# Lo parts of the attention keys or queries kept on both partition halves, in a two-block transformer kernel on one Trainium2 core

## The chip, the core and the metric

The kernel runs on one core of a Trainium2 chip. Its time is the device time of one execution in microseconds (us), taken as the median of several runs; lower is better.

## The reference, cut to what matters

Batch 1, 512 tokens, model width 1024, all in float32. A first block mixes a linear recurrence with a dilated attention of 8 heads; a second block of two layers follows, each with an attention mixer and a mixture of 16 experts. The even layer's mixer has 4 differential heads (two score sets each) and 8 grouped-query heads over 512 tokens plus 256 context tokens; the odd layer's has 16 heads whose score is a sum of a 64-wide and a 32-wide product. All scores are products over a head dimension of 64:

```python
def diff_attend(q, k, v, lam, scale):
    s = jnp.einsum('bqhcd,bkhcd->bhcqk', q, k).astype(jnp.float32) * scale
...
def gqa_attend(q, k, v, scale):
    s = jnp.einsum('bqhgd,bkhd->bhgqk', q, k).astype(jnp.float32) * scale
...
def mla_attend(qn, qr, kn, kr, v, scale):
    s = jnp.einsum('bqhd,bkhd->bhqk', qn, kn) + jnp.einsum('bqhr,bkr->bhqk', qr, kr)
```

## The kernel before

**Split products.** Large products are made of parts: a value w becomes hi, its copy in the type fp32r, and lo = w - hi, also fp32r. A dense product is three matmuls, hi by hi, hi by lo and lo by hi (`mm3`, L318 to L320). In the attention, with a head dimension of 64, the two parts of a vector lie one above the other on the 128 partitions that a matmul contracts over.

**Stacks.** `stack_pair` (L456) puts, for two heads, hi on one partition half and lo on the other. `stack_keys` (L484) takes the other operand of two heads: `kh[j]` holds the hi part of head j twice, on both halves (two ScalarE copies, L493 and L494), while `kl` holds the lo parts of both heads in one tile, head 0 on the lower half and head 1 on the upper (one VectorE subtraction each, L495). `dup_head` (L468) does the same for one key head that several query heads share, but writes its lo part on both halves (L475, L476); the grouped-query heads use it.

**Scores.** A unit is one head (or one of the two score sets of a differential head) of one tile of 128 queries. Its scores are sums of passes in PSUM (`scores`, L497 to L504, keys in chunks of 512 and 256): the full stack against the doubled hi part (128 rows: hi times hi and lo times hi), then only the half of the stack that holds hi against the lo part (64 rows). The odd layer has a third pass, the 32-wide product, also 128 rows (`qp`, `krs`), and there queries and keys have changed roles: the stack is `ks`, the lo tile is `ql`. The first block writes the two passes out by itself (L817, L818).

```python
passes.append(((qh[b], ks[b]), (ql[sl], ks[b][sl]), (qp[b], krs)))
```

**What follows the scores.** VectorE takes the maximum (L511), ScalarE the exponential (L514), TensorE transposes the result (L525, copied out at L252 or L254), and TensorE multiplies by the values (L533 or L1146). `Pipe` emits the later steps of a unit two units behind its scores. At the same time `weave` spreads the next heads' projections (L318 to L320, evacuated by ScalarE), their norms and stacks, and matmuls for the modulation vectors (L359, weights streamed by DMA) between the attention steps. The engines' final orders come from a scheduler at build time.

**Between the stages.** The end of each attention loads the out-projection's weights (`resident_`, L305): eight rows `wo_raw` [128, 1024] through two buffers, each split by ScalarE (L267) and GpSimd (L268). Behind them on the same SP queue are the first loads of the experts' weights (`we`, L1418, 1 MB each). Then come the out-projection with the router, and the experts. The order of the program is: first block (0 to 415 us of the profile), even mixer (415 to 873), its out-projection (to about 1000), experts (to 1600), odd mixer (1600 to 1985, attention from 1670), its out-projection, experts (2080 to the end).

Of the kernel before, what the change touches and what calls it, by code (L numbers as in the profile page):

```python
# [19 lines left out]
D = 1024  # L20
# [82 lines left out]
class Pipe:  # L103
    """Units of work in three stages, the later stages emitted `lag` units after the first."""
# [20 lines left out]
def weave(*streams):  # L125
    """Steps of several (generator, its number of steps), spread evenly."""
    live = [[0.5 / max(n, 1), 1.0 / max(n, 1), g] for g, n in streams]
    while live:
        x = min(live, key=lambda z: z[0])
        if next(x[2], True) is None:  # L130
            x[0] += x[1]
            yield
        else:
            live.remove(x)
# [7 lines left out]
def drain(gen):  # L142
    """Runs gen; returns what it returns."""
# [14 lines left out]
class Kernel:  # L158
# [20 lines left out]
    def pbank(self):  # L179
        """A bank that may be held between steps."""  # L180
# [46 lines left out]
    def rsqrt(self, ssq, n, scale, eps=EPS, engine=None, tag="rs"):  # L227
        """1 / sqrt(ssq * scale + eps) [128, n] by Newton's iteration, on VectorE or mostly on another engine."""
# [19 lines left out]
    def evac(self, out, ps, act=4, of=6):  # L248
        """PSUM to SBUF, on ScalarE in `act` of `of` cases."""
# [20 lines left out]
    def group_(self, src):  # L270
        """The parts of a group of weights, in steps of one piece; each is split two steps after its load."""
# [25 lines left out]
    def transposed_(self, ps, hT, w, c0):  # L297
        """transposed() into ps, in two steps"""
# [6 lines left out]
    def resident_(self, src, pool, js, out, mod=8, raw=None):  # L305
        """The rows js (tiles of 128) of src [128, 8, 1024], split, to out[j], in steps."""
        for j in js:
            i = j % mod
            w = (raw or pool).tile([128, D], F32, name="wo_raw", tag="xr", bufs=2)
            self.nc.sync.dma_start(out=w, in_=src[:, j, :])  # L310
            hi, lo = (pool.tile([128, D], F32R, name=f"wo_{nm}{i}", bufs=1) for nm in ("hi", "lo"))
            self.split(hi, lo, w)
# [9 lines left out]
    def natural_(self, ps, h, w, c0, n):  # L322
        """ps [128 tokens, n] = h @ w[:, c0:c0+n], in two steps; h: the two parts [128, k, 128 tokens]."""
# [7 lines left out]
    def ada(self, w, b, stat, nmod, nvec, pool, ring, banks, done, bank=None, bufs=None):  # L331
        """Steps; done(mods, rows) is called with every two modulations' rows: rows holds at partition
        32 t + m the columns (4 bank + t) * 512 of vector m."""
# [34 lines left out]
    def ada_cols(self, rows, n, dst, mods, nvec):  # L368
        """dst[:, m, j, :] = the 8 columns of modulation mods[j] of vector m."""
# [23 lines left out]
    def ada2(self, i):  # L393
        """Modulation of layer i: columns of the mixer's scale and shift, the rows in DRAM, and the
        steps of some banks of it."""
# [20 lines left out]
    def tile_rstd(self, x, junk):  # L416
        """1 / rms of the rows of x [128, 1024]; junk: a tile to write over."""
# [4 lines left out]
    def normalise(self, xs, xn, junk):  # L422
        """Two token tiles [128, 1024] to xn; junk: a tile to write over."""
# [8 lines left out]
    def build_hT(self, xn, A, B, hi, lo, pool):  # L432
        """Two normalised token tiles, modulated, transposed and split, to hi and lo [128, 8, 256]."""
# [22 lines left out]
    def stack_pair(self, S0, S1, nat, ntt, bank=None):  # L456
        """nat(t) [128 tokens, 2 heads x 64]: S0 = hi | lo of the first head, S1 = lo | hi of the second."""
# [10 lines left out]
    def dup_head(self, H, L, ps, r, s):  # L468
        """H, L [128, .]: twice the hi and twice the lo parts of ps, on partitions r.."""
# [14 lines left out]
    def stack_keys(self, kh, kl, nat, ntt, bank=None):  # L484
        """nat(t) [128 tokens, 2 heads x 64]: kh[j] = twice the hi part of head j, kl = the lo parts of both."""
        a_, v = self.nc.scalar, self.nc.vector
        for t0 in range(0, ntt, 4)[::-1]:
# [3 lines left out]
            for j in range(2):  # L491
                q, o = slice(64 * j, 64 * j + 64), slice(64 - 64 * j, 128 - 64 * j)
                a_.activation(kh[j][q, s], ps[q], AF.Copy)  # L493
                a_.activation(kh[j][o, s], ps[q], AF.Copy)  # L494
                v.tensor_sub(kl[q, s], ps[q], kh[j][q, s])  # L495

    def scores(self, passes, q0, k0, k1):  # L497
        """PSUM [128 queries from q0, keys k0..k1] summed over pairs (query stack, key stack)."""
# [1326 lines left out]
```

## Time and profile before

| | |
|---|---|
| median of 3 runs | 2590.11 us (2589.2 to 2593.87) |
| profiled execution | span 2592.4 us |
| TensorE (PE) busy | 2247.1 us, 87% |
| VectorE (DVE) busy | 1052.2 us, 41% |
| ScalarE (ACT) busy | 710.7 us, 27% |
| GpSimd (POOL) busy | 580.7 us, 22% |
| mean granted TensorE clock | 0.928 of full speed |

The span runs from the first to the last instruction of the profiled execution; no time of its own beyond the span is given for it, and it lies within the three runs. PE is the matmul, PEld the load of its stationary operand, which may run beside another matmul. A matmul's recorded duration contains its latency, so consecutive rows overlap; the pace of TensorE is read from the distance between starts.

### The profile page before, as it was taken

The numbers are of one execution on the slowest core, as the hardware profiler recorded it, in microseconds if no ns is written. First come the engines' busy times: TensorE is split into PE (matmuls) and PEld (weight loads), VectorE is DVE, ScalarE is ACT, GpSimd is POOL, SyncE is SP. The second block draws the span as 40 slices with busy tenths as digits, with TensorE's granted clock in tenths as the row PEclk, the third lists the DMA queues.
The fourth block names the chain that finished last, engine by engine and source line by source line (L and its number), as shares of the span: only waits on it lengthen the run. The fifth ranks groups of instructions, "written<-read, shape, count | busy, mean of one in ns | idle before, by whom it ended". The sixth has DMA issues, their size and how long they took to land.

```text
span 2592.4 us, 32517 instructions
## 1 busy us (share of the span) xinstructions
PE 2247.1 (87%) x12298; PEld 1226.4 (47%) x12298; DVE 1052.2 (41%) x2745; ACT 710.7 (27%) x1626; POOL 580.7 (22%) x788
## 2 busy tenths in 40 slices
PE   5999878999999986999999996699999688776777
PEld 1767667676777771222222224466666532222222
DVE  5365677544767653111111116777673610000000
ACT  3355543334544320000000004345555100000000
POOL 3343231331333321011111003333233110000000
PEclk7999888998998897999999998699999889998889
DMA  7531231322332458999999953032214699999997
GB/s 276 163 115 41 78 122 42 122 71 69 113 94 75 162 206 292 383 382 377 377 377 383 388 189 94 21 98 83 70 42 141 253 348 389 397 396 397 389 402 283
DMA packets 158456, 563.85 MB, mean 217 GB/s; under 512 B 16198, under 2 KB 16454, under 8 KB 158172
## 3 DMA queue, kind: packets, MB, share of 16 engines
q1 hardware_dynamic: 143868, 522.90, 54.2%
q0 software_dynamic: 14432, 38.88, 5.5%
q8 instruction: 97, 1.59, 0.2%
q14 instruction: 59, 0.48, 0.1%
HBM read 538.59 MB, written 23.14 MB: 217 GB/s over the span
## 4 chain that ended last, share of the span: by engine, by line
PE 39%; DMA 14%; DVE 5%; ACT 3%; issue 3%; POOL 0%; SPq 0%; POOLq 0%; ACTq 0%; DVEq 0%
PE bank L1470 12%; DMA we<-in_w_exp_gate_dram 9%; PE pbank L1505 5%; PE bank L503 5%; PE bank L1461 5%; DMA we<-in_w_exp_up_dram 4%; PE pbank L1520 2%; PE bank L533 2%; PE bank L525 1%; PE pbank L318 1%; PE pbank L320 1%; PE pbank L359 1%; PE pbank L319 1%; PE pbank L1316 1%; PE pbank L1483 1%
## 5 line engine op out<-in xcount | busy, mean ns | idle before, releaser
L1470 PE MATMUL bank<-we,XT 128*64 128x512 f32 x2048 | 506.8, 627 | 95.7 <-DMA we<-in_w_exp_gate_dram 69.8
L1470 PEld LDWEIGHTS bank<-we,XT 128*64 128x64 f32 x2048 | 140.8, 142 | 442.4 <-issue 324.1
L1480 DVE TENSOR_TENSOR sg<-sg,bank 128x512 f32<-128x512 f32 x32 | 22.0, 687 | 644.5 <-PE bank L1470 644.5
L1505 PE MATMUL pbank<-we,hT 128*64 128x512 f32 x1024 | 229.1, 596 | 10.7 <-ACT hT L1485 9.0
L1479 ACT ACTIVATE sg<-bank 128x512 f32<-128x512 f32 x32 | 19.1, 597 | 658.6 <-PE bank L1470 658.6
L511 DVE TENSOR_REDUCE mx<-bank 128x1 f32<-128x768 f32 (+1 forms) x160 | 135.6, 848 | 106.5 <-PE bank L503 105.9
L1441 POOL DMA_INDIRECT X<-H,gx x32 | 29.9, 934 | 615.9 <-PE bank L1447 551.7
L514 ACT ACTIVATE p<-bank,mx 128x768 f32<-128x768 f32 (+1 forms) x160 | 130.5, 817 | 69.8 <-DVE mx L511 23.7
L525 PE MATMUL bank<-cons,p 128*128 128x128 f32 x800 | 130.5, 289 | 14.2 <-ACT pT L252 6.1
L503 PE MATMUL bank<-ks,qs 128*128 128x256 f32 (+2 forms) x320 | 131.5, 459 | 11.3 <-ACT p L514 4.5
L1505 PEld LDWEIGHTS pbank<-we,hT 128*64 128x64 f32 x1024 | 71.5, 137 | 145.6 <-issue 126.2
L1461 PE MATMUL bank<-we,XT 128*32 128x512 f32 x1024 | 133.4, 604 | 0.0
L268 POOL TENSOR_TENSOR lo<-w,hi 128x1024 fp32r<-128x1024 f32 (+1 forms) x44 | 94.7, 2159 | 102.8 <-ACT hi L267 83.6
L525 PEld LDWEIGHTS bank<-cons,p 128*128 128x128 f32 x800 | 94.1, 147 | 45.0 <-ACT pT L252 12.4
L252 ACT ACTIVATE pT<-bank 128x256 f32<-128x256 f32 (+3 forms) x187 | 84.4, 476 | 105.3 <-PE bank L525 98.8
L318 PE MATMUL pbank<-hi,h 128*128 128x384 f32 x288 | 101.5, 353 | 7.2 <-DVE mix L954 3.0
L503 PEld LDWEIGHTS bank<-ks,qs 128*128 128x128 f32 (+1 forms) x320 | 64.4, 201 | 77.8 <-issue 47.2
L320 PE MATMUL pbank<-hi,h 128*128 128x384 f32 x288 | 99.4, 345 | 0.0
L319 PE MATMUL pbank<-lo,h 128*128 128x384 f32 x288 | 98.9, 343 | 0.0
L1509 DVE SCALAR_TENSOR_TENSOR yl<-pbank,gt,m 128x512 f32<-128x512 f32 x32 | 23.9, 748 | 178.1 <-PE pbank L1505 151.7
L268 POOL TENSOR_TENSOR wo_lo<-wo_raw,wo_hi 128x1024 fp32r<-128x1024 f32 x24 | 57.2, 2392 | 92.5 <-ACT wo_hi L267 92.4
L1461 PEld LDWEIGHTS bank<-we,XT 128*32 128x32 f32 x1024 | 21.8, 108 | 101.2 <-issue 101.2
(445 smaller groups left out, 4204.1 us busy)
## 6 DMA issues: line engine op xcount, KB each, us to landing
we<-in_w_exp_down_dram SPq DMA_DIRECT2D x127, 1024.0 KB
we<-in_w_exp_up_dram SPq DMA_DIRECT2D x124, 1024.0 KB
we<-in_w_exp_gate_dram SPq DMA_DIRECT2D x123, 1024.0 KB
wa<-in_w_ada_dram SPq DMA_DIRECT2D x120, 512.0 KB
w<-in_w_in_dram SPq DMA_DIRECT2D x24, 512.0 KB
w<-in_w_in_even_dram SPq DMA_DIRECT2D x20, 384.0 KB
H<-h SPq DMA_DIRECT2D x10, 512.0 KB
we<-in_w_exp_gate_dram POOLq DMA_DIRECT2D x5, 1024.0 KB, 10.4
```

The source lines that it names most:

```text
L252: self.nc.scalar.activation(out, ps, AF.Copy)
L268: (engine or self.nc.gpsimd).tensor_sub(lo, w, hi)
L318: t.matmul(ps, lhsT=lhs[0], rhs=rhs[0], start=start, stop=False)
L319: t.matmul(ps, lhsT=lhs[0], rhs=rhs[1], start=False, stop=False)
L320: t.matmul(ps, lhsT=lhs[1], rhs=rhs[0], start=False, stop=stop)
L503: self.nc.tensor.matmul(ps[:, a - k0:b - k0], lhsT=qs[:, q0:q0 + 128], rhs=ks[:, a:b], start=i == 0, stop=i == len(passes) - 1)
L511: nc.vector.tensor_reduce(m, ps, axis=AX, op=OP.max, negate=True)
L514: nc.scalar.activation(p, ps, AF.Exp, bias=m, accum_out=den)
L525: self.nc.tensor.transpose(ps[:, a - b:a - b + 128], p[:, a:a + 128], self.ident)
L1461: nc.tensor.matmul(pc[q:q + 32], lhsT=XT[:, k, 64:96], rhs=w[:, k % 2, 512 * h:512 * h + 512], start=k == 0, stop=k == 7)
L1470: nc.tensor.matmul(ps[64 * h:64 * h + 64], lhsT=XT[:, k, :64], rhs=w[:, k - k0, 512 * h:512 * h + 512], start=k == 0, stop=k == 7)
L1505: nc.tensor.matmul(py[64 * h:64 * h + 64], lhsT=hT[:, j, 64 * kh:64 * kh + 64], rhs=w[:, 512 * h:512 * h + 512], start=j == 0 and kh == 0, ...
```

## The change

`stack_keys` now calls `dup_head` for both of its heads, so the lo part of each head stands on both partition halves in a tile of its own. Every score pass then uses the whole stack against it, 128 rows. The score gains the product of the two lo parts, which was left out before. The lo tiles take more memory: the even mixer's ring of key tiles goes from 5 to 6 buffers, the first block and the odd mixer keep two lo tiles per pair in place of one. The out-projections of the second block load `wo_raw` in pieces of 512 columns in place of 1024 (two loads and two splits per row), and the even mixer's grid table is loaded over a scratch tile (`t1`) of the projection.

```diff
     def stack_keys(self, kh, kl, nat, ntt, bank=None):
-        a_, v = self.nc.scalar, self.nc.vector
         for t0 in range(0, ntt, 4)[::-1]:
             t1 = min(ntt, t0 + 4)
             ps = self.to_psum(nat, t0, t1, 128, bank)
             s = slice(t0 * 128, t1 * 128)
             for j in range(2):
-                q, o = slice(64 * j, 64 * j + 64), slice(64 - 64 * j, 128 - 64 * j)
-                a_.activation(kh[j][q, s], ps[q], AF.Copy)
-                a_.activation(kh[j][o, s], ps[q], AF.Copy)
-                v.tensor_sub(kl[q, s], ps[q], kh[j][q, s])
+                self.dup_head(kh[j], kl[j], ps[64 * j:64 * j + 64], 64 * j, s)
...
     def resident_(self, src, pool, js, out, mod=8, raw=None):
         for j in js:
             i = j % mod
-            w = (raw or pool).tile([128, D], F32, name="wo_raw", tag="xr", bufs=2)
-            self.nc.sync.dma_start(out=w, in_=src[:, j, :])
+            n = D if raw else 512
+            parts = []
+            for c in range(0, D, n):
+                w = (raw or pool).tile([128, n], F32, name="wo_raw", tag="xr", bufs=2)
+                self.nc.sync.dma_start(out=w, in_=src[:, j, c:c + n])
+                parts.append((slice(c, c + n), w))
             hi, lo = (pool.tile([128, D], F32R, name=f"wo_{nm}{i}", bufs=1) for nm in ("hi", "lo"))
-            self.split(hi, lo, w)
+            for c, w in parts:
+                self.split(hi[:, c], lo[:, c], w)
...
-            kl = stk.tile([128, S], F32R, name="kl", bufs=1)
+            kl = [stk.tile([128, S], F32R, name="kl") for _ in range(2)]
...
-                    nc.tensor.matmul(ps[:, :nn], lhsT=qs[b][sl, q], rhs=kl[sl, :nn], start=False, stop=True)
+                    nc.tensor.matmul(ps[:, :nn], lhsT=qs[b][:, q], rhs=kl[b][:, :nn], start=False, stop=True)
...
-            return [stk.tile([128, S + C], F32R, name=tag, bufs=5 if tag == "ks" else 4) for _ in range(n)]
+            return [stk.tile([128, S + C], F32R, name=tag, bufs=6 if tag == "ks" else 4) for _ in range(n)]
...
-                self.att_pair(pipe, [((qs[b], kh), (qs[b][64 * b:64 * b + 64], kl[64 * b:64 * b + 64]))
-                                     for b in range(2)], t, k0, S + C, lambda i, b: vt[:, i],
+                self.att_pair(pipe, [((qs[b], kh), (qs[b], kl)) for b in range(2)], t, k0, S + C,
+                              lambda i, b: vt[:, i],
...
-                    a, den, r = self.softmax(self.scores([(qs[c], kh[c]), (qs[c][sl], kl[sl])], t * 128, k0, S + C),
-                                             n, pp)
+                    a, den, r = self.softmax(self.scores([(qs[c], kh[c]), (qs[c], kl[c])], t * 128, k0, S + C), n, pp)
...
-            kh, (kl,), qs = tiles("ks", 2), tiles("ks", 1), tiles("qs", 2)
+            kh, kl, qs = tiles("ks", 2), tiles("ks", 2), tiles("qs", 2)
...
-        self.load_grid(64, ta.tile([128, 512], F32, name="grid64"))
+        self.load_grid(64, pj.tile([128, 512], F32, name="t1", bufs=1))
...
-            ql = stk.tile([128, S], F32R, name="ql")
+            ql = [stk.tile([128, S], F32R, name=f"ql{b}") for b in range(2)]
...
-                sl = slice(64 * b, 64 * b + 64)
-                passes.append(((qh[b], ks[b]), (ql[sl], ks[b][sl]), (qp[b], krs)))
+                passes.append(((qh[b], ks[b]), (ql[b], ks[b]), (qp[b], krs)))
```

**What moves on VectorE.** One stretch of VectorE's order in the odd mixer where the stacks of a pair are built between the maxima (`mx`) of another pair. Before:

```order
1741 L511 TENSOR_REDUCE mx<-bank_13505 128x1
1742 L495 TENSOR_TENSOR ql<-pbank,qh_13458 64x512
1743 L1723 TENSOR_TENSOR kn<-kn,pr_o 128x256
1744 L516 RECIPROCAL rden<-den 128x1
1745 L1743 TENSOR_TENSOR qp_13463<-pbank,qp_13463 64x512
1746 L511 TENSOR_REDUCE mx<-bank_13530 128x1
1747 L495 TENSOR_TENSOR ql<-pbank,qh_13459 64x512
```

The same place of the changed kernel:

```order
1768 L512 TENSOR_REDUCE mx<-bank_13575 128x1
1769 L480 TENSOR_TENSOR ql_13527<-pbank,qh_13525 64x512
1770 L1721 TENSOR_TENSOR kn<-kn,pr_o 128x256
1771 L481 TENSOR_TENSOR ql_13527<-pbank,qh_13525 64x512
1772 L517 RECIPROCAL rden<-den 128x1
1773 L1741 TENSOR_TENSOR qp_13531<-pbank,qp_13531 64x512
1774 L512 TENSOR_REDUCE mx<-bank_13600 128x1
1775 L517 RECIPROCAL rden<-den 128x1
1776 L480 TENSOR_TENSOR ql_13528<-pbank,qh_13526 64x512
1777 L481 TENSOR_TENSOR ql_13528<-pbank,qh_13526 64x512
```

Each head's lo subtraction is now two, of the same shape; 40 are added in the whole program (8 in the first block, 16 in the even, 16 in the odd mixer).

**What moves on SP.** The end of the even mixer's attention on SP, the queue that issues the loads. Before, all eight rows of `wo_raw` and then the experts' first weights (`we`):

```order
97 L310 DMA wo_raw<-in_w_out_even_0_dram 128x1024 x8
98 L1418 DMA we_9486<-in_w_exp_gate_dram 128x2x1024
99 L1418 DMA we_9488<-in_w_exp_up_dram 128x2x1024
100 L1418 DMA we_9526<-in_w_exp_gate_dram 128x2x1024
101 L1418 DMA we_9528<-in_w_exp_up_dram 128x2x1024
102 L1418 DMA we_9506<-in_w_exp_gate_dram 128x2x1024
103 L1418 DMA we_9508<-in_w_exp_up_dram 128x2x1024
104 L1786 DMA x<-x1d 128x1024
```

The changed kernel, from the first `we` on, behind 13 of the 16 half rows:

```order
97 L1416 DMA we_9550<-in_w_exp_gate_dram 128x2x1024
98 L1416 DMA we_9552<-in_w_exp_up_dram 128x2x1024
99 L313 DMA wo_raw<-in_w_out_even_0_dram 128x512
100 L1416 DMA we_9590<-in_w_exp_gate_dram 128x2x1024
101 L1416 DMA we_9592<-in_w_exp_up_dram 128x2x1024
102 L313 DMA wo_raw<-in_w_out_even_0_dram 128x512
103 L1416 DMA we_9570<-in_w_exp_gate_dram 128x2x1024
104 L1416 DMA we_9572<-in_w_exp_up_dram 128x2x1024
105 L313 DMA wo_raw<-in_w_out_even_0_dram 128x512
106 L1783 DMA x<-x1d 128x1024
```

The last three half rows now stand behind two, four and six of the 1 MB loads. In the odd mixer all 16 half rows stay ahead of the experts' loads. TensorE has the same matmuls in number; the 64-row ones are now 128-row.

## Rows read from the trace of the kernel before

**Rows 1.** Windows: stretch; busy of PE, PEld, DVE, ACT, POOL; clock, DMA share, GB/s.

```profile
150.00:280.00 130.00, 128.35 (x687) 96.77 (x686) 74.16 (x202) 68.97 (x140) 35.59 (x36) 1.00 0.21 67
415.00:873.00 458.00, 427.97 (x2443) 309.11 (x2444) 279.49 (x720) 203.58 (x526) 133.76 (x207) 0.92 0.27 86
1670.00:1985.00 315.00, 299.04 (x2016) 198.24 (x2016) 208.34 (x573) 168.50 (x421) 105.20 (x265) 0.98 0.24 76
...
800.00:873.00 73.00, 60.55 (x252) 43.72 (x252) 61.02 (x138) 39.84 (x98) 28.97 (x25) 0.71 0.19 58
```

**Rows 2.** Chain of waits, odd attention, 1670 to 1985 us: shares of that stretch.

```profile
by line: PE bank L503 39.3%; PE bank L533 12.7%; PE bank L525 7.7%; PE pbank L359 6.6%; PE pbank L318 3.7%; PE pbank L453 3.1%; PE pbank L319 2.9%; PE pbank L320 2.9%; ACT p L514 2.6%; ACT pT L252 2.4%; issue 2.1%; PE bank L556 1.7%; DVE pT
```

**Rows 3.** Waits, 1670 to 1985: who waited for whom, us in total, times, longest.

```profile
DVE mx L511 <- PE bank L503: 58.6, 57, 2.4
PEld bank L503 <- issue: 52.6, 207, 0.8
```

**Rows 4.** Timeline of PE, odd attention: start us, duration us, instruction; rows*columns loaded, shape streamed.

```profile
1757.02 0.29 PE L320 MATMUL pbank<-wkv,ckv 128*128 128x256 f32 x1
1757.14 0.48 PE L503 MATMUL bank<-ks,qh 128*128 128x512 f32 x1
1757.55 0.49 PE L503 MATMUL bank<-ks,ql 64*128 64x512 f32 x1
1757.97 0.49 PE L503 MATMUL bank<-krs,qp 128*128 128x512 f32 x1
...
1759.05 0.38 PE L525 MATMUL bank<-cons,p 128*128 128x128 f32 x2
```

**Rows 5.** Timeline of PEld, the same unit.

```profile
1756.90 0.19 PEld L320 LDWEIGHTS pbank<-wkv,ckv 128*128 128x128 f32 x1
...
1757.54 0.18 PEld L503 LDWEIGHTS bank<-ks,ql 64*128 64x128 f32 x1 [0.24 <-issue]
```

**Rows 6.** Timeline of PE, out-projection: two 128-row matmuls that follow one another.

```profile
878.16 0.40 PE L319 MATMUL bank<-wo_lo,yhi 128*128 128x512 f32 x1
878.39 0.40 PE L320 MATMUL bank<-wo_hi,ylo 128*128 128x512 f32 x1
```

**Rows 7.** Timeline of PE, even attention: one unit of four passes, and what follows.

```profile
807.13 1.53 PE L503 MATMUL bank<-ks,qs 128*128 128x512 f32 x4
808.60 0.44 PE L453 MATMUL pbank<-cons,qk 128*128 128x128 f32 x2
```

**Rows 8.** Timeline of PE, first block: a 64-row pass, and the next unit's.

```profile
142.81 0.38 PE L818 MATMUL bank<-kl,qs 64*128 64x256 f32 x1
...
143.43 0.38 PE L818 MATMUL bank<-kl,qs 64*128 64x256 f32 x1
```

**Rows 9.** Groups by form, whole span: the 64-row passes of the even mixer.

```profile
L503 PE MATMUL bank<-ks,qs 64*128 64x256 f32 x96 | 39.6, 413 | 0.0
L503 PE MATMUL bank<-ks,qs 64*128 64x512 f32 x64 | 34.4, 538 | 3.9 <-DVE ks L495 3.9
```

**Rows 10.** Line L495: duration ns min/median/max, first and last start, forms.

```profile
L495 DVE TENSOR_TENSOR ks<-pbank,ks x16: 405/555/695, 595.7 to 834.6; 64x256 fp32r<-64x256 f32 x8, 64x512 fp32r<-64x512 f32 x8
L495 DVE TENSOR_TENSOR ql<-pbank,qh x16: 662/689/695, 1663.0 to 1946.8; 64x512 fp32r<-64x512 f32 x16
```

**Rows 11.** Groups by form, 800 to 873 us: the 64-row passes there.

```profile
L503 PE MATMUL bank<-ks,qs 64*128 64x256 f32 x17 | 8.2, 481 | 0.0
L503 PE MATMUL bank<-ks,qs 64*128 64x512 f32 x12 | 8.0, 667 | 3.9 <-DVE ks L495 3.9
```

**Rows 12.** Timeline of PE, end of the even attention: one unit of four passes.

```profile
848.82 2.52 PE L503 MATMUL bank<-ks,qs 128*128 128x512 f32 x4
```

**Rows 13.** Timeline of SP's queue: first and sixth issue of experts' weights.

```profile
873.23 0.38 SPq L1418 DMA_DIRECT2D we<-in_w_exp_gate_dram  x1
...
883.03 0.37 SPq L1418 DMA_DIRECT2D we<-in_w_exp_up_dram  x1
```

**Rows 14.** Windows view, the start of the out-projection (columns as in rows 1).

```profile
873.00:890.00 17.00, 17.00 (x72) 13.64 (x72) 4.55 (x17) 2.69 (x7) 4.18 (x4) 0.92 0.93 366
```

More of the change, by code (lines that the diff above doesn't have):

```diff
@@ L1127, in first @@
                 def first(c, t=t, k0=k0, n=n, p=p, dens=dens, rs=rs):
-                    sl = slice(64 * c, 64 * c + 64)
-                    a, den, r = self.softmax(self.scores([(qs[c], kh[c]), (qs[c][sl], kl[sl])], t * 128, k0, S + C),
-                                             n, pp)
+                    a, den, r = self.softmax(self.scores([(qs[c], kh[c]), (qs[c], kl[c])], t * 128, k0, S + C), n, pp)
                     p.append(a)
@@ L1748, in stacks @@
             for b in range(2):
-                sl = slice(64 * b, 64 * b + 64)
-                passes.append(((qh[b], ks[b]), (ql[sl], ks[b][sl]), (qp[b], krs)))
+                passes.append(((qh[b], ks[b]), (ql[b], ks[b]), (qp[b], krs)))
             cur["a"] = passes, vn
```

## The prediction, made before the changed kernel was run

> **What bounds the kernel now.** I read the windows view first, because the change touches only the three attention stages. In the first block's middle, the even attention and the odd attention TensorE is busy 99%, 93% and 95% of the time, VectorE 57%, 61% and 66% [rows 1]. The experts and out-projections have no score matmul and only move with what comes before them. A recorded matmul holds its latency, so I checked with the chain of waits that TensorE really sets the end: in the odd attention 39.3% of 315 us, 123.8 us, lies on the score line L503 alone [rows 2]. There are 64 units (8 pairs, 4 tiles, 2 heads), and one takes 1.91 us from its first pass to the next work [rows 4]; 64 x 1.91 = 122 us. So every unit's scores are on the path. The waits view says the same from the other side: VectorE's longest wait is for the scores, 58.6 us in 57 waits [rows 3].
>
> Then the timeline of one unit, to see what its 1.91 us hold. Ahead of it 128-row matmuls of 256 columns follow at 0.12 us (1757.02 to 1757.14); those of 512 columns at 0.23 us [rows 6]. Inside the unit, the 64-row pass starts 0.41 us after a 512-column pass, and the next 128-row pass 0.42 us after that [rows 4]. The weight loader shows why: the load for L320 starts at 1756.90, 0.12 us ahead of its own matmul and while another runs; the load of the 64-row pass starts at 1757.54, after 0.24 us of idle, together with its matmul [rows 4, 5]. A change between 128 and 64 rows makes the load wait until the array is empty. The loader lost 52.6 us in 207 such waits in this stage [rows 3].
>
> **The change, part by part.** *64-row passes become 128-row.* No change of row count is left inside a unit. I price a 128-row lo pass by its neighbours, 0.23 us for 512 columns and 0.12 us for 256.
> - Odd: 3 x 0.23 + 3 x 0.12 = 1.05 us in place of 1.91; 0.86 x 64 = 55.0 us.
> - Even: a unit of four passes takes 1.47 us (807.13 to 808.60) [rows 7], and would take 0.70; 64 such units (64 passes of 512 columns [rows 9]) give 49.3 us. The other 96 - 64 = 32 units (context queries) have two passes of 256 columns, 0.62 us from one lo pass to the next [rows 8], 0.24 after; 0.38 x 32 = 12.2 us.
> - First block: 32 units at the same 0.38, 12.2 us (longer shapes change rows just as often).
>
> That is 129 us of TensorE. What of it reaches the end differs by stage.
>
> *Odd, 41 us.* All 55 us are on the path, until another engine replaces TensorE. VectorE gets 16 more subtractions of 0.689 us [rows 10], 11.0 us: 208.3 + 11.0 = 219.3 us of work [rows 1]. With all 55 us gone the stage would be 260 us and VectorE 84% busy. The only stretch where it is that busy now is the even attention's tail, 61.0 of 73 us [rows 1]. I take 80%, 274 us: a gain of 41. Bounds: 55, and 23 (VectorE at 75%, half way between 66% and 84%).
>
> *Even, 43 us.* Of the 61.5 us, 12 x 0.77 + 5 x 0.38 = 11.1 belong to the tail from 800 us on [rows 11]. Before it, VectorE has 279.5 - 61.0 = 218.5 us of work in 385 us [rows 1] and gets 12 subtractions of 0.555 us [rows 10] more: 225 us. With 50.4 us gone, it would be busy 67%, the share at which the odd stage has TensorE on the path today. So I take 43 of the 50; bounds 30 and 50. In the tail VectorE is already the busier one and TensorE waits 3.9 us for the lo subtraction itself [rows 11], which is now doubled: 0, with bounds -2 (the four subtractions of the last head) and +11.
>
> *First block, 8 us.* TensorE is busy 128 of 130 us and VectorE 57% [rows 1], so most of the 12 should arrive; no chain is shown for this stage, so I take two thirds, 8, with bounds 0 and 12. The 8 subtractions there hide in the 43% in which VectorE is free; without that cover they cost 8 x 0.689 = 5.5 us.
>
> *SP's queue at the end of the even attention, -5 us.* The last half row of the weights is issued behind six loads of 1.05 MB. The first of these is issued at the end of the attention, 873.2 us, the sixth at 883.0 [rows 13]. At 366 GB/s [rows 14] 6.3 MB take 17.2 us, the half row 0.7 more. The first tile's 48 matmuls take 11.0 us at 0.23; row 7 is wanted after 42, at 9.7 us, and 12 matmuls of the second tile that are now ordered ahead cover 2.8. So some 5 us of waiting; bounds 0 and 8 (no cover).
>
> *At nothing:* the 16 extra loads and splits of half rows, the same bytes, behind the attention's last heads (in the odd stage all of them are ahead of the experts' loads; if that cover goes, the price is that of the term above once more); the grid table over `t1`, whose user is the third group of heads, two groups later; the sixth key buffer, no instruction. ScalarE has the same number of copies in the stacks.
>
> Sum: 41 + 43 + 0 + 8 - 5 = 87 us. The profiled execution's span is 2592.4 us, 2.3 above the median of 2590.1, with nothing known around it; 2592.4 - 87 = 2505.4, as a median **2503 us**.
>
> **A rule that speaks against it.** The rows show a 128-row load running beside another 128-row matmul [rows 4, 5]. The Trainium skill, "TensorE: Matmul & The Clock Gate", section "What overlaps and what doesn't", says that a weight load overlaps with running matmuls only where the row groups differ. By that rule a 128-row lo pass would hide its load no better than a 64-row one, and the sum would be -5. The measured pace of 0.12 us decides against it here.
>
> **The rivals.**
> 1. *VectorE replaces TensorE* (gain 25 to 65, about 2545). In its favour: 84% in the odd stage, subtractions put between maxima, so that a maximum, and with it the exponential and TensorE's transposes, comes later. Against: 58.6 us of its idle time are waits for just these scores. At the lower bounds 23 + 30 - 2 + 0 - 5 = 46.
> 2. *Everything arrives* (gain 110 or more, about 2475): 55 + 50 + 12 less small losses; for it, that every odd unit is on the path.
> 3. *The weight loads stay exposed*: the unit keeps its 1.91 us and the change doesn't do what it could; 2595 with the queue's 5 us. Against it the rows above. The skill's section just named would have it so.
> 4. *The clock falls* (slower). A four-pass unit's record is 1.53 us at full speed [rows 7] and 2.52 in the tail [rows 12], 1.65 times, where the granted clock averaged 0.71 (the 1.2 GHz level in 58% of the time) with TensorE busy 83% [rows 1]. The odd stage has 0.98 at 95%; after the change it would be busy about (299 - 55) / 274 = 89%, between the two. The shortened stages, 274 + 342 = 616 us, become 616 / (1 - 0.39 f) if a share f of the time is spent at 1.2 GHz; from f = 0.33 on this takes back the 87 us and 0.2% besides. At f = 0.45 it costs 131 us: 2590 - 87 + 131 = 2634. Against it: only the tail, where VectorE holds TensorE up, shows such a share.
>
> **How the numbers follow.** Forecast (gain 65 to 110) 0.58, rival 1 0.20, rival 2 0.15, rival 3 0.03, rival 4 0.04. A measurement of this kernel tells about 0.2% (5 us) from no change. Faster are the forecast and rivals 1 and 2: 0.93; rival 3 is the same, 0.03; rival 4 slower, 0.04. With every term at its best the gain is 128 us (2462), at its worst 43 (23 + 30 - 2 + 0 - 8, so 2547). I let the range reach from 2468, which cuts off a third of rival 2, to 2547, which leaves out the weakest part of rival 1 and rivals 3 and 4: some 0.17 outside.
>
> **What would show it.** Right: the odd unit at about 1.05 us from its first pass to the next work, the even one at 0.70; no idle "issue" of the weight loader before the lo pass; some 274 us for the odd attention where it was 315; VectorE busy about 80% there; a wait of TensorE on `wo_lo` of row 7 near the end of the even attention, some 5 us. Wrong: a lo pass still 0.4 us behind its neighbour (rival 3); TensorE's idle time before L525 or L533 grown by as much as the scores shrank (rival 1); a granted clock in the odd attention well below 0.9 (rival 4); or the stages shorter and the end not, which would mean that something between the stages, such as the loads of weights, took it back.

## The result, and the profile after

The changed kernel takes **2520.0 us** (median of 4 runs, 2514.4 to 2525.7) against 2592.0 us before (4 runs, 2589.2 to 2595.9): a ratio of **0.972, 95% interval 0.970 to 0.974**, 72 us less. The forecast was 2503 us; the range, 2468 to 2547, holds the result. The profiled execution took 2520.2 us, with a span of 2518.4.

**Where the time went.** I cut both traces at the same events: the starts of the first score pass of the even mixer, of the first matmul on `wo`, of the first on `we`, and of the first and the last score pass of the odd mixer. Lengths in us:

| stretch | before | changed | difference | forecast |
|---|---|---|---|---|
| start to the first even score pass (holds the first block) | 417.4 | 411.8 | -5.6 | -8 |
| even attention | 455.3 | 410.2 | -45.1 | -43 |
| even out-projection, to the first expert's matmul | 125.0 | 134.9 | **+9.9** | +5 |
| experts, and on to the first odd score pass | 673.4 | 675.8 | +2.4 | 0 |
| odd attention, first to last score pass | 314.1 | 276.9 | -37.2 | -41 |
| the rest | 607.2 | 608.8 | +1.6 | 0 |
| span | 2592.4 | 2518.4 | -74.0 | -87 |

So the attention stages did nearly what was forecast, and 10 us were given back in a stage without a score matmul.

The windows view of the changed kernel answers to [rows 1] (same columns): a stretch of the first block, the even attention, its tail (from VectorE's 80th maximum `mx` of the even mixer on), the odd attention. The last row is the kernel before, its even tail from the same maximum on.

```profile
140.00:278.00 138.00, 131.49 (x740) 102.94 (x739) 93.87 (x238) 75.80 (x156) 44.66 (x43) 0.99 0.25 77
412.00:822.00 410.00, 364.44 (x2437) 293.25 (x2438) 282.18 (x730) 200.79 (x529) 134.20 (x212) 0.96 0.30 96
761.40:822.10 60.70, 40.50 (x231) 32.65 (x228) 56.32 (x132) 38.75 (x102) 24.67 (x27) 0.86 0.25 74
1633.00:1910.00 277.00, 251.64 (x2012) 194.15 (x2011) 213.95 (x586) 167.44 (x424) 102.72 (x269) 0.98 0.26 84
...
803.60:872.80 69.20, 56.75 (x230) 40.20 (x231) 58.85 (x132) 39.21 (x96) 26.17 (x22) 0.70 0.20 61
```

In the odd stage TensorE is busy 91% (95% before) and VectorE 77% (66%; 80% were forecast). The granted clock is 0.98 in the odd attention as before. In the even one it has risen, from 0.92 to 0.96, and in its tail from 0.70 to 0.86.

One odd unit in the timeline of TensorE (columns as in [rows 4]), and the first rows of the next one, which follows transposes:

```profile
1781.49 0.28 PE L325 MATMUL pbank<-wkv,ckv 128*128 128x256 f32 x1
1781.61 0.39 PE L504 MATMUL bank<-ks,qh 128*128 128x512 f32 x1
1781.84 0.40 PE L504 MATMUL bank<-ks,ql 128*128 128x512 f32 x1
1782.07 0.39 PE L504 MATMUL bank<-krs,qp 128*128 128x512 f32 x1
1782.30 0.28 PE L504 MATMUL bank<-ks,qh 128*128 128x256 f32 x1
1782.42 0.28 PE L504 MATMUL bank<-ks,ql 128*128 128x256 f32 x1
1782.54 0.28 PE L504 MATMUL bank<-krs,qp 128*128 128x256 f32 x1
1782.66 0.82 PE L526 MATMUL bank<-cons,p 128*128 128x128 f32 x6
1783.49 0.50 PE L504 MATMUL bank<-ks,qh 128*128 128x512 f32 x1
1783.83 0.39 PE L504 MATMUL bank<-ks,ql 128*128 128x512 f32 x1
```

From 1781.61 to 1782.66 are the forecast 1.05 us, with every pass at 0.23 or 0.12. But the second unit needs 0.34 for its first pass, and that is the usual case: the median over the 45 units that stand in one piece is 1.15 us (before: 1.93 over 48). The weight loader's timeline, the lo pass and the next of the first unit:

```profile
1781.61 0.19 PEld L504 LDWEIGHTS bank<-ks,ql 128*128 128x128 f32 x1
1781.84 0.19 PEld L504 LDWEIGHTS bank<-krs,qp 128*128 128x128 f32 x1
```

The load for the lo pass (1781.61) now starts 0.23 us ahead of that pass, beside the running matmul, where it had to wait 0.24 us [rows 5]. The even unit of four passes, 1.47 us in [rows 7], is 0.90 us here (604.81 to 605.71; 0.70 forecast); the median is 0.81 over the 42 that stand in one piece, where it was 1.48 over 44 before:

```profile
604.81 0.96 PE L504 MATMUL bank<-ks,qs 128*128 128x512 f32 x4
605.71 0.76 PE L534 MATMUL bank<-pT,vt 128*64 128x128 f32 x9
```

The waits of the odd attention, which answer to [rows 3]:

```profile
DVE mx L512 <- PE bank L504: 14.3, 28, 2.0
...
PEld bank L526 <- ACT pT L252: 9.9, 13, 2.4
...
PEld bank L504 <- issue: 4.6, 19, 0.8
```

The loader's stall went from 52.6 us to 4.6, VectorE's wait for scores from 58.6 to 14.3. In the chain of waits the score line holds 14.8%, where it held 39.3% [rows 2], and no line has taken its place as the one bound:

```profile
by line: PE bank L504 14.8%; PE bank L534 8.5%; issue 6.2%; DMA wo_raw<-in_w_out_odd_dram 5.1%; DVE mx L512 4.9%; PE bank L526 4.8%; PE pbank L364 4.5%; DMA wa<-in_w_ada_dram 3.6%; ACT p L515 3.2%; PE pbank L323 3.1%; ACT pT L252 3.0%; POOL
```

**What was given back.** SP's queue at the end of the even attention (start, duration, instruction) shows the order that the change made: half rows of `wo_raw` behind experts' loads.

```profile
818.08 0.46 SPq L1416 DMA_DIRECT2D we<-in_w_exp_up_dram  x1
818.63 0.42 SPq L313 DMA_DIRECT2D wo_raw<-in_w_out_even_dram  x1
...
822.02 0.34 SPq L313 DMA_DIRECT2D wo_raw<-in_w_out_even_dram  x1
...
827.01 0.37 SPq L1416 DMA_DIRECT2D we<-in_w_exp_up_dram  x1
829.33 0.34 SPq L313 DMA_DIRECT2D wo_raw<-in_w_out_even_dram  x1
```

And TensorE's timeline in the out-projection, where the last row is wanted:

```profile
839.68 0.50 PE L323 MATMUL bank<-wo_hi,yhi 128*128 128x512 f32 x1 [0.36 <-ACT wo_hi L267]
843.93 0.79 PE L324 MATMUL bank<-wo_lo,yhi 128*128 128x512 f32 x1 [3.75 <-POOL wo_lo L268]
...
846.46 0.63 PE L323 MATMUL bank<-wo_hi,yhi 128*128 128x512 f32 x1
846.89 0.63 PE L324 MATMUL bank<-wo_lo,yhi 128*128 128x512 f32 x1
```

TensorE stops 3.75 us for the last lo part. The row was late, but the stop has a second cause. ScalarE had the hi part done at 839.62 us, and GpSimd made the lo part only at 842.60, behind other work of its own (timelines of ScalarE and GpSimd):

```profile
839.01 0.61 ACT L267 ACTIVATE wo_hi<-wo_raw 128x512 fp32r<-128x512 f32 x1
...
839.18 1.28 POOL L268 TENSOR_TENSOR ylo<-Y,yhi 128x512 fp32r<-128x512 f32 x1 [4.10 <-ACT yhi L267]
840.41 1.27 POOL L1280 TENSOR_TENSOR x<-x,u 128x512 f32<-128x512 f32 x1
841.97 0.60 POOL L1298 DMA_DIRECT2D cacc<-x  x1 [0.30 <-POOL x L1280]
842.60 1.27 POOL L268 TENSOR_TENSOR wo_lo<-wo_raw,wo_hi 128x512 fp32r<-128x512 f32 x1
```

So 3.0 us of the stop are GpSimd's order. Behind the stop a matmul takes 0.43 us from start to start instead of 0.23: the granted clock has fallen to the 1.2 GHz level (0.50), and some 35 us later it does so once more (windows view):

```profile
843.20:849.80 6.60, 5.58 (x12) 3.97 (x13) 2.05 (x7) 1.78 (x3) 2.92 (x3) 0.50 0.19 74
...
884.20:887.40 3.20, 3.20 (x9) 2.44 (x8) 2.97 (x7) 0.00 (x0) 0.58 (x1) 0.50 0.12 19
```

### The profile page after: what moved, and what is told of

Same layout as the page of the kernel before. It is cut to its first block, busy times and chain, and to the rows that moved or that the text cites. A ratio compares the mean times of both kernels' runs of the same rounds, so it can differ in the third digit from the quotient of the medians.

```text
span 2518.4 us, 32647 instructions
## 1 busy us (share of the span) xinstructions
PE 2134.2 (85%) x12298; PEld 1209.4 (48%) x12298; DVE 1074.1 (43%) x2785; ACT 711.5 (28%) x1642; POOL 586.6 (23%) x804
## 5 line engine op out<-in xcount | busy, mean ns | idle before, releaser
L512 DVE TENSOR_REDUCE mx<-bank 128x1 f32<-128x768 f32 (+1 forms) x160 | 134.9, 846 | 35.8 <-PE bank L504 34.5
L526 PEld LDWEIGHTS bank<-cons,p 128*128 128x128 f32 x800 | 92.4, 143 | 61.0 <-ACT pT L252 17.6
L504 PE MATMUL bank<-ks,qs 128*128 128x256 f32 (+1 forms) x320 | 83.4, 375 | 12.5 <-ACT p L515 9.1
L268 POOL TENSOR_TENSOR wo_lo<-wo_raw,wo_hi 128x512 fp32r<-128x512 f32 (+1 forms) x40 | 60.7, 1527 | 99.6 <-ACT wo_hi L267 97.5
L504 PEld LDWEIGHTS bank<-ks,qs 128*128 128x128 f32 x320 | 57.1, 205 | 35.3 <-ACT p L515 14.5
L1483 ACT ACTIVATE hT<-pbank 128x512 f32<-128x512 f32 x32 | 19.1, 597 | 183.5 <-PE pbank L1481 183.5
```

Source lines behind the costliest of these rows:

```text
L268: (engine or self.nc.gpsimd).tensor_sub(lo, w, hi)
L504: self.nc.tensor.matmul(ps[:, a - k0:b - k0], lhsT=qs[:, q0:q0 + 128], rhs=ks[:, a:b], start=i == 0, stop=i == len(passes) - 1)
L512: nc.vector.tensor_reduce(m, ps, axis=AX, op=OP.max, negate=True)
L526: self.nc.tensor.transpose(ps[:, a - b:a - b + 128], p[:, a:a + 128], self.ident)
```

## The experiments

The length of the stages in every profiled execution, cut as above (us; "start" is to the first even score pass), and the times. Each ratio is to the runs of before made beside that kernel, whose medians lie between 2592.0 and 2597.4 us:

| kernel | start | even | out-proj. | odd | median | ratio to before, 95% |
|---|---|---|---|---|---|---|
| before | 417.4 | 455.3 | 125.0 | 314.1 | 2592.0 | 1 |
| changed | 411.8 | 410.2 | 134.9 | 276.9 | 2520.0 | 0.972 (0.970 to 0.974) |
| e1 two changes | 419.3 | 429.5 | 123.9 | 284.5 | 2537.7 | 0.977 (0.974 to 0.980) |
| e2 64 rows | 415.7 | 459.5 | 123.4 | 318.5 | 2602.5 | 1.004 (1.002 to 1.006) |
| e5 odd 64 | 409.8 | 412.4 | 135.9 | 320.2 | 2562.1 | 0.987 (0.985 to 0.990) |
| e4 rows first | 409.3 | 413.2 | 124.8 | 277.0 | 2504.7 | 0.966 (0.963 to 0.968) |
| e6 GpSimd copy | 410.4 | 414.9 | 125.0 | 271.1 | 2505.9 | 0.965 (0.964 to 0.967) |
| e7 third sub. | 410.3 | 418.9 | 123.5 | 285.0 | 2522.3 | 0.972 (0.970 to 0.973) |
| e8 ScalarE copy | 408.6 | 401.9 | 129.5 | 275.5 | 2499.5 | 0.963 (0.961 to 0.964) |
| e9 evacuations | 410.8 | 420.3 | 125.7 | 273.9 | 2511.2 | 0.968 (0.966 to 0.969) |
| e10 mixed | 410.3 | 403.8 | 125.7 | 272.7 | 2498.4 | 0.962 (0.959 to 0.964) |
| e11 changed again | 410.2 | 410.9 | 135.9 | 279.2 | 2521.4 | 0.970 (0.968 to 0.972) |

The same stage, unedited, differs by up to 2 or 3 us between executions (the changed kernel and e11: 276.9 and 279.2), so smaller differences are not read.

**E1: is it the change of row count, or the 64-row matmul?** The kernel before, with the passes in another order:

```diff
-        for a in range(k0, k1, 512):
-            b = min(k1, a + 512)
-            for i, (qs, ks) in enumerate(passes):
+        cols = [(a, min(k1, a + 512)) for a in range(k0, k1, 512)]
+        full = [p for p in passes if p[0].shape[0] == 128]
+        half = [p for p in passes if p[0].shape[0] == 64]
+        for part in (full, half):
+            for a, b in cols:
+                for qs, ks in part:
...
```

> The kernel before, with one thing moved: in a unit of the even and the odd mixer all 128-row passes of both column chunks come first and the 64-row passes last, so that the row count changes twice in a unit and not four times. The matmuls are the same in number and shape, VectorE's work is that of before. My theory (each change of row count empties TensorE's array and costs about 0.86 / 4 = 0.21 us): the odd unit goes from 1.91 to about 1.48 us, the even one from 1.47 to about 1.09; 64 x 0.43 = 27.5 us of TensorE in the odd stage, (64 - 12) x 0.385 = 20 us in the even stage before its tail. VectorE has room, so nearly all arrives: 40 to 48 us less than before, about 2548. Rival A (a 64-row matmul is slow in itself, wherever it stands): no change, 2592 within 5. Rival B (VectorE takes the end over as soon as scores come sooner): half of it, about 2570.

The unit's timeline (odd mixer, from its first pass to the next unit's), and the loader's wait in the whole stage:

```profile
1758.86 0.50 PE L506 MATMUL bank<-ks,qh 128*128 128x512 f32 x1
1759.20 0.40 PE L506 MATMUL bank<-krs,qp 128*128 128x512 f32 x1
1759.44 0.28 PE L506 MATMUL bank<-ks,qh 128*128 128x256 f32 x1
1759.55 0.28 PE L506 MATMUL bank<-krs,qp 128*128 128x256 f32 x1
1759.76 0.61 PE L506 MATMUL bank<-ks,ql 64*128 64x512 f32 x2
1760.30 0.50 PE L506 MATMUL bank<-ks,qh 128*128 128x512 f32 x1
1760.64 0.39 PE L506 MATMUL bank<-krs,qp 128*128 128x512 f32 x1
```

```profile
PEld bank L506 <- issue: 6.4, 28, 0.8
```

The same six matmuls take 1.44 us (median 1.42) in place of 1.93: 0.25 us for each of the two changes that are gone, a little over the 0.21 I had worked out. The two that are left, at the unit's edges, are worth 1.42 - 1.15 = 0.27 us together against the changed kernel, since a unit's first pass mostly comes late there too (0.34 us, as shown above). Where the 64-row load follows 128-row work, the pass comes 0.09 us late (1759.55 to 1759.76 instead of 0.12). Rival A is out: the same 64-row matmuls stand in a unit that is 0.49 us shorter, and a 64-row pass of 512 columns takes 0.34 us to the next 64-row one (1759.76 to 1760.10, inside the x2), as much as a 128-row pass takes behind a change (1760.30 to 1760.64). Rival B is out as well: the odd stage gives 29.6 us, nearly all of 64 x 0.49 = 31 us, for VectorE has got no more work. The whole gained 57 us (2537.7 against 2595.0 of the runs of before beside it), more than the 40 to 48 expected: 29.6 in the odd stage and 25.8 in the even one, 4 of them in its tail, for which nothing had been expected.

**E2: does anything else in the change gain?** The changed kernel with the lo passes cut back to 64 rows in all three stages:

```diff
...
-                passes.append(((qh[b], ks[b]), (ql[b], ks[b]), (qp[b], krs)))
+                sl = slice(64 * b, 64 * b + 64)
+                passes.append(((qh[b], ks[b]), (ql[b][sl], ks[b][sl]), (qp[b], krs)))
```

> The changed kernel with every lo pass of the scores (first block, even, odd) cut back to 64 rows; the doubled lo tiles, the 40 added subtractions and the loads by half rows stay. My theory: the whole gain lies in the passes, and what stays costs little while TensorE sets the end: the odd unit is 1.91 us again, the odd attention 314 to 320 us, the whole 2592 to 2606. In this kernel's order only one half row stands behind one load of an expert, so the queue's term is nearly absent. Rival A (the rest of the change pays for part of the gain, for instance by another order): below 2585. Rival B (VectorE's added work is on the path already): 2606 to 2617, since 16 x 0.689 + 12 x 0.555 + 8 x 0.689 = 23 us of it would then be added nearly whole.

The waits of its odd attention:

```profile
DVE mx L512 <- PE bank L504: 56.1, 54, 2.2
PEld bank L504 <- issue: 53.1, 209, 0.8
```

Both stalls are back at their size of [rows 3], and the whole gain is gone. What is left of the change costs 4.4 us in the odd attention (6.1 in E5 below, whose odd stage is the same) and 4.2 us in the even one. TensorE is busy 94% of the odd stage there, and still 40 to 55% of the 11.0 us of added subtractions seem to arrive; with 2 or 3 us between executions this is no more than a rough share, and that it is the subtractions was not shown. Against this kernel the passes alone are worth 459.5 - 410.2 = 49.3 us in the even and 318.5 - 276.9 = 41.6 us in the odd attention.

**E5: do the stages add?** The same edit in the odd mixer alone.

> The changed kernel with only the odd mixer's lo pass cut back to 64 rows. My theory (the stages' gains add): the odd attention goes from 276.9 back to 314 us or a little more, everything else keeps the changed kernel's time, so 2520 + 37 to 41 = 2557 to 2561. Rival (in the odd stage VectorE with its 11 us of added work bounds already, so the pass matters less than the difference of the traces says): 2535 to 2545.

The odd attention takes 320.2 us, the rest is the changed kernel's; the median, 2562.1 us, is 42 us above it and 1 us above the expected range. The stages add, and the rival is out.

**E4: is it the queue?** The changed kernel with the experts' first six loads ordered behind the last half row (`last_row` is the DMA that `resident_` issued last):

```diff
...
+        elif self.nload <= 6:
+            with self.tc.issue_after(self.last_row.ins):
+                self.nc.sync.dma_start(out=t, in_=src)
```

> The changed kernel with the first six loads of the experts' weights put behind the last half row of the out-projection's weights on SP; nothing else is edited. My theory: the out-projection after the even attention took 134.8 us against 124.9 before because row 7 came late (TensorE waits 3.75 us for its lo part at 843.9 us and then runs at a granted clock of 0.80 in that stretch). With the half rows first it returns to 125 to 128 us, and the whole to 2510 to 2514, 6 to 10 below the changed kernel (ratio to before 0.968 to 0.970). Rival A (the loads are bound by bandwidth, 410 GB/s there, whatever their order, and the experts' weights now come late instead): the stretch up to the experts' first matmul keeps its length, 2520 within 4. Rival B (the shorter attention has lost its tail's cover and the time is VectorE's): the same, 2520, but with no wait for the lo part.

The windows of the out-projection in the changed kernel (its start, the stretch of the wait, the whole):

```profile
822.00:834.00 12.00, 11.75 (x54) 9.39 (x54) 3.61 (x20) 3.22 (x8) 2.79 (x3) 1.00 1.03 409
834.00:849.00 15.00, 10.60 (x34) 7.46 (x33) 2.08 (x4) 2.93 (x5) 7.70 (x7) 0.80 0.24 94
822.00:957.00 135.00, 96.33 (x457) 77.09 (x458) 73.03 (x204) 22.75 (x49) 38.46 (x38) 0.82 0.52 191
```

and in this one:

```profile
822.00:834.00 12.00, 12.00 (x51) 9.70 (x50) 4.86 (x16) 3.58 (x9) 5.10 (x4) 0.86 0.73 272
834.00:849.00 15.00, 15.00 (x66) 12.16 (x65) 9.39 (x19) 3.08 (x6) 6.54 (x6) 1.00 0.77 305
822.00:947.00 125.00, 92.15 (x457) 75.82 (x455) 74.89 (x200) 22.75 (x49) 38.39 (x38) 0.84 0.57 212
...
822.50:825.30 2.80, 2.80 (x9) 2.22 (x9) 1.13 (x2) 1.69 (x5) 1.41 (x2) 0.50 0.20 74
```

From 834 to 849 us TensorE did 34 matmuls, and 66 here. Of the 10 us, 38.67 - 32.85 = 5.8 are TensorE's idle time; the other 96.33 - 92.15 = 4.2 are the same 457 matmuls taking longer. Both kernels spend the last 36 to 39 us of the stage at the 1.2 GHz level; ahead of that the changed one has 6.6 us of it behind the stop and 3.2 us later on, this one only the first 2.8 us. The out-projection is 124.8 us again, as before the change. Rival A is out: the transfer of the six loads costs nothing where it starts later. So is rival B, for VectorE's work is the same. The median fell by 15 us, more than this stage explains; beside E11, the changed kernel once more, it is 17. The stages were cut in an execution that took 2509.0 us, 4 above this kernel's median, so that they show 11; the other 4 to 6 us are not explained.

> The changed kernel once more, unedited, beside the same runs of before, so that its distance to e4_rows_first rests on more than four runs. By my theory the first six loads of experts' weights ahead of the last half rows cost 10 to 11 us (134.8 against 124.8 us of out-projection): 2515 to 2520, ratio 0.969 to 0.973. Rival (e4_rows_first is faster for another reason, up to 15 us by the medians so far): above 2520, or at 2508 and below if its first four runs were high.

It took 2521.4 us with an out-projection of 135.9 us: the give-back is there again. The time itself lies 1.4 us above the expected range, where the rival had put it; that E4 gains by something else besides is therefore not excluded.

**E7: what does VectorE's added work cost now?** From here on the base is E4. One more subtraction of the same values:

```diff
         v.tensor_sub(L[o, s], ps, H[q, s])
+        v.tensor_sub(L[o, s], ps, H[q, s])
```

> The kernel of e4_rows_first with the second subtraction of each lo tile made twice (the same values written again): the suspected price of VectorE's added work once more, 16 x 0.689 = 11.0 us in the odd stage, 12 x 0.555 = 6.7 in the even one, 8 x 0.689 = 5.5 in the first block. Where TensorE bounded (all lo passes at 64 rows against the kernel before) the same work cost 4.4 us in the odd and 4.2 us in the even attention. Theory (VectorE is now the co-bound): more of it arrives, 7 to 11 in the odd stage, 4 to 7 in the even one: 2505 + 11 to 18 = 2516 to 2523. Rival (VectorE's total does not matter, its work lies in gaps): 2505 to 2511.

The time, 2522.3 us, is the theory's. The odd stage takes 8.0 us more, 73% of the added 11.0; in E2 and E5 it was 40 to 55%. The even stage takes 5.7 us more. There I had counted too little: this line also serves the two groups that doubled their lo keys before the change, so 20 subtractions of 0.56 us are added, 11.2 us; 51% of them arrive, as 4.2 of 16 x 0.56 = 9.0 us (47%) did in E2. That VectorE has come up to TensorE in the odd stage is not shown by this. The odd windows of E4 and of this kernel:

```profile
1622.00:1899.00 277.00, 250.85 (x2011) 193.62 (x2011) 214.46 (x586) 167.41 (x424) 102.42 (x269) 0.98 0.26 84
1628.00:1913.00 285.00, 255.41 (x2012) 196.24 (x2013) 229.81 (x600) 169.28 (x426) 103.35 (x271) 0.97 0.25 82
```

TensorE's idle time has grown by 3.4 us; the other 4.6 are longer matmuls, at a granted clock of 0.97 where it was 0.98.

**E6, E8, E10: the copy on another engine.** The second half of each lo tile is copied from the first, by GpSimd (E6), by ScalarE (E8), or by ScalarE in the first block and the even mixer and by GpSimd in the odd one (E10):

```diff
-        v.tensor_sub(L[o, s], ps, H[q, s])
+        self.nc.gpsimd.tensor_copy(L[o, s], L[q, s])
```

> The kernel of e4_rows_first, with the second half of each lo tile copied from the first by GpSimd in place of VectorE's second subtraction: VectorE does the work of before again. Theory (behind the row-count changes VectorE is the co-bound: the odd stage has TensorE 252 and VectorE 215 us busy of 278, and the two maxima and the stacks stand in one queue): the odd attention falls from 277 to 270 to 273 us, the even one by 3 to 4 us, the first block by 0 to 1; 2505 - 8 to 13 = 2492 to 2497. Rival A (the rest of the expected gain is lost between ScalarE, VectorE and TensorE in the loop over two score banks, whatever VectorE's total is): 2505 within 4. Rival B (the copies come late on GpSimd, and the scores wait for them): above 2509.

> As e6_pool_copy, but the copy is made by ScalarE: VectorE loses 11.0 us in the odd stage, ScalarE (167 us busy of 278 there) gets as much. Theory (VectorE is the co-bound and ScalarE has room): 2497 to 2502, a little behind the copy on GpSimd since ScalarE's exponentials set when a score bank comes free. Rival (ScalarE carries that loop): slower than e4_rows_first, 2507 to 2515.

> The kernel of e4_rows_first with VectorE's second subtraction replaced by a copy of the first: by ScalarE in the first block and the even mixer (where e8_act_copy has attention and out-projection together 6.6 us shorter than e4_rows_first), by GpSimd in the odd mixer (where e6_pool_copy has 5.9 us less). Theory (the two stages don't know of one another, the copies take VectorE's added work off the path in both): 2505 - 12 = about 2493, ratio to before 0.959 to 0.962. Rival (the gains of e8_act_copy and e6_pool_copy are chance of two schedules): 2499 to 2506.

E6 gives the theory's number in the odd stage alone (271.1 us, -5.9). In the even one it gains nothing (+1.7), and the whole, 2505.9 us, is no faster than E4, as rival A had it. E8 gains in the even stage (-11.3, of which the out-projection, +4.7, gives part back) and little in the odd one (-1.5); its 2499.5 us lie in the theory's range, but not for the odd stage, on which the theory rested. E10 takes the better of both: 403.8 and 272.7 us, 2498 us in all, 6 us below E4 by the medians and 11 by the ratios to before, where 12 were expected. Its interval (0.959 to 0.964) lies below that of the changed kernel and of E11, and overlaps that of E8 and a little that of E4. So it is faster than both kernels compared here; its lead over E4 is likely but not shown, and one over E8 (2499.5 us) can't be told. The odd stage at VectorE's old load:

```profile
1624.60:1895.70 271.10, 244.68 (x2011) 190.85 (x2011) 208.09 (x572) 167.77 (x423) 110.34 (x283) 0.99 0.26 85
```

That is E6's window: VectorE 208.1 us as before the change (208.3, [rows 1]), and TensorE still idle for 26 us of 271, as in E4 (26 of 277). So the 5.9 us are matmul time, at a granted clock of 0.99 (0.98 in E4), and TensorE's idle time has not shrunk. VectorE's total is then not what keeps the rest of the gain away, and what made E6's odd stage shorter stays open.

**E9: a lighter VectorE by another way.** More of the evacuations from PSUM on ScalarE:

```diff
-    def evac(self, out, ps, act=4, of=6):
+    def evac(self, out, ps, act=5, of=6):
```

> The kernel of e4_rows_first with five of six instead of four of six evacuations from PSUM on ScalarE (the transposed weights of the softmax above all): in the odd stage about 20 x 0.55 = 11 us move from VectorE to ScalarE, in the even one about as much, in smaller shapes. Theory (VectorE is the co-bound): 2495 to 2501. Rival (a transposed tile that waits on ScalarE behind an exponential costs more than VectorE gains): 2505 or above.

Odd 273.9 us (-3.1), even 420.3 (+7.1). The median, 2511.2 us, is the rival's and 6 above E4, though the intervals of the two ratios overlap. So it did not pay to take just any work off VectorE. That in the even stage transposed tiles wait behind ScalarE's exponentials, as the rival has it, was not shown.

## Why the prediction was right, and where its sizes were off

**The mechanism was right.** It is the change of row count, not the 64 rows, that a unit pays for: E1 takes half of the changes away and 0.51 of the 0.78 us of a unit go, E2 puts all of them back and the whole price returns. The pace of [rows 6], 0.23 and 0.12 us, is what a lo pass takes now. Rival 3 falls by the loader's rows. The Trainium skill, "TensorE: Matmul & The Clock Gate", section "What overlaps and what doesn't", lets a load overlap only with a matmul on other row groups; the trace disagrees, with 128-row loads that start 0.12 and 0.23 us ahead of their pass beside 128-row matmuls. The Trainium skill, "TensorEngine Tiling (Array Packing)", section "Key Properties", says of the array's modes that changing between them drains it, without a price; E1 agrees that a change costs, at 0.25 us for one in the odd unit. Rival 4, the clock, did not come: in the odd attention it stayed at 0.98, in the even one it rose.

**The sizes**, by the prediction's own steps:
- *Odd, 41; measured 37.2.* The 55 us of TensorE were 6 too many: a unit was priced as if its first pass always followed wide 128-row work, 1.05 us, and it mostly follows transposes or the products with the values, 1.15; 64 x (1.93 - 1.15) = 50. TensorE's busy time fell by 300.6 - 251.6 = 48.9 us against E2. Its idle time rose by 7 (from 18.4 of 319 us to 25.4 of 277): its waits for transposed tiles to be copied out went from 7.6 to 11.9 us, those for `qp` from 0.8 to 3.4. What E2 keeps of the change took 4.4: 48.9 - 7 - 4.4 = 37.5. So rival 1 had a part of the truth. VectorE is busy 77%, near the 80% that I took, but that VectorE's total is the reason is not borne out: with its old load back (E6) TensorE is idle as long as before.
- *Even, 43 and 0 for the tail; measured 45.1*, 49.3 against E2. The sum came out near by errors that cancel, which is luck. The passes give less than the 61.5 us: a unit of four passes fell from 1.48 to 0.81 us (0.77 forecast, 0.67 measured), one of two from 0.62 to 0.43 in the median (0.24 forecast), so 64 x 0.67 + 32 x 0.19 = 49. TensorE's busy time fell by 428.0 - 364.4 = 63.5 us all the same, as the granted clock rose from 0.92 to 0.96, which was not forecast; its idle time rose by 15.5. And the gain stands elsewhere: 36.7 us ahead of the 80th maximum, where 43 were forecast, and 8.5 in the tail, where none was. What made the clock rise there was not tested.
- *First block, 8; measured 5.6*, which the difference between executions hardly separates from 8 (E4, E5 and E11, with the same first block: 8.1, 7.6 and 7.2).
- *SP's queue, -5 with bounds 0 and 8; measured -9.9. This is the step that failed.* The wait itself came out near, 3.75 + 0.36 us, by two errors that cancel: row 7 was reached 17.6 us after the out-projection's first matmul (839.7 - 822.1; 12.5 forecast), with 74 matmuls ahead of it where 54 had been counted, and its lo part came 21.8 us after it (17.9 forecast). The transfer was priced about right, for the hi part was there at 17.6 us. The split stood at nothing, and GpSimd took it up 3.0 us late, behind other work. What the step left out besides is what follows a stop: 4.2 us of longer matmuls. With some 1.5 us of other idle time that is the 9.9.
- *At nothing* stood 0 for the stretches in between; they took 2.4 + 1.6 us more. In E4 these two differ from before by 1.4 and 0.8, so part of it goes with the queue or is scatter.

Sum: 45.1 + 37.2 + 5.6 - 9.9 - 4.0 = 74 us of span, 72 of the medians, against 87.

## What to carry to other kernels

Look at the row counts of neighbouring matmuls: where 64- and 128-row ones alternate, each change inside a unit cost about as much as a pass of 512 columns, and simply ordering them by row count (E1, no memory and no added work) bought four fifths of what doubling the operand did. When a change splits a load into smaller ones, read the new order of the queue, and that of the engines that work on what was loaded: here three half rows that slipped behind 1 MB loads cost 10 us, and one ordering rule got them back. A stop of TensorE can cost more than its length: here 5.8 us more of idle time came with 4.2 us of longer matmuls. Compare parts and not only sums: the even stage came out near its forecast, with a gain in its tail and a higher clock that the prediction did not have.

## What the runs showed that I had not expected

- What the change adds beside the passes, mostly work on VectorE, seems to cost 40 to 55% of that work's length even where TensorE is busy 94% and VectorE 68% (E2, E5): a share of busy time tells little about it. What does was not shown.
- The even attention runs at a higher granted clock once its scores are faster (0.96 against 0.92), and the odd stages of E4, E6 and E7, with the same passes, differ as much by the length of their matmuls as by TensorE's waits.
- The same copy is worth 5.9 us on GpSimd and 1.5 on ScalarE in the odd stage, and the other way round in the even one (no gain on GpSimd, 11.3 us on ScalarE before the out-projection takes some back). E10 repeats the better of both (-4.3 and -9.4 us against E4); the reason stays open.
